# Gates and gated branches of an encoder layer with tokens on partitions, nine of their row pairs as seven products

## The chip, the cores and the metric

The kernel runs on one core of a Trainium2 chip. The core has TensorE (PE in the profile; its weight loads, which overlap its products, are PEld), VectorE (DVE), ScalarE (ACT), GpSimd (POOL) and SyncE (SP), which issues nearly all DMA transfers here. What counts is the device time of one execution in microseconds; a kernel's time is the median of its runs.

## The reference

One layer of an encoder: 256 tokens, 2048 channels, everything in float32.

```python
h = rms_norm(x, norm_mix_pre)
proj = h @ w_in                       # 10240 columns
qa, ka, va, qn, kn, vn, gates = split(proj)     # 6 x 1024 columns, then 2 x 2048 of gates
oa = rms_norm(diff_attention(rope(qa), rope(ka), va)) * (1 - lambda_init)    # [256, 1024]
on = neighbourhood_attention(qn, kn, vn)                                     # [256, 1024]
g_a, g_b = split(sigmoid(gates))                                             # [256, 2048] each
mixed = g_a * (oa @ w_branch_a) + g_b * (on @ w_branch_b)
x = x + rms_norm(mixed @ w_out)
u = square(relu(rms_norm(x) @ w_up))            # 8192 columns
x = x + rms_norm(u @ w_down)
```

The change concerns the lines with gates, g_a, g_b and mixed.

## The kernel before

**Two parts.** Each float32 matrix is two float32r tiles, hi (a cast of it, by ScalarE) and lo (the remainder, by VectorE), and a product is taken as hi·hi + hi·lo + lo·hi. Activations are kept transposed, with channels on the partitions: hT is eight tiles hT0 to hT7 for two 128-row chunks each, every chunk as 256 tokens of hi and then 256 of lo. The attention's results are kept alike, as oaT and onT, eight chunks each. The factor of the row norm, rx, is not in hT; it is multiplied in when a product's result is taken out of PSUM.

**Weights.** load (L94) fetches four 128-row chunks of 512 columns, 1 MB, with one DMA issued by SP, into a raw buffer; split (L101) makes hi (L115, ScalarE) and lo (L116, VectorE) of it in two pieces of 1024 elements a partition. The pool wp has three buffers each for raw, hi and lo. So the next load waits until the remainder of the load three before it has been taken, and a remainder needs its hi first.

**Products.** Two forms are in use. wgroup (L183) holds the weights still and moves the activations: for each 128 of its 512 output columns and each chunk, one product moves hi and lo of the activations past hi of the weights, 512 columns (L191), and one moves hi past lo of the weights, 256 columns (L192). The result is transposed, channels on partitions, in the two halves of a PSUM bank, which halves (L251) adds: ScalarE copies one, VectorE adds the other (L256). agroup (L220) holds the activations still and moves the weights: three products of 512 columns for each chunk and each 128 tokens (L229 to L231). Its result has tokens on the partitions and no halves to add. v of the attention and the output projection use agroup, the down projection the same products (L777 to L779); q, k, gates, branches and the up projection use wgroup. PSUM has eight banks, four under the name mm (large groups) and four under ms (everything else).

**The stage that is changed.** A loop runs over four column groups cg of 512 channels. Each has four wgroup calls: gate a (tiles ga_p, ga_h, ga_l, with the group's number behind ga: 16 chunks, four loads), gate b (gb, the same), branch a (ba: 8 chunks, two loads) and branch b (bb). gate_evac adds the halves, multiplies by rx as a row over all tokens (rxb, L603) and takes the sigmoid (L604); br_evac adds the halves and multiplies with the gate. At the end of a column group the two gated branches are added (L618) and split into mh and ml (L619, L620). They have channels on the partitions, so the output projection's agroup (groups y0 to y3, mstat at L624) uses them as they are.

**Order.** The program is written group by group. advance (L171) puts pieces of the open attention heads between a group's chunks; advance(99) in the loop finishes them. The Tile framework's scheduler then sets each engine's order with a simulated timeline, so that instructions of neighbouring groups mix; each engine, and the queue of SP, takes its own in that order. Tiles come from pools with fixed numbers of buffers: pages (27 of 4 KB a partition) for hT, oaT, onT, gates and the like, wp for weights, tmp for the attention's small tiles (six of 1 KB, seven of 2 KB), tiny, and the two pools of banks.

## Time and profile before

| | |
|---|---|
| median of three runs | 1397.59 us (1396.96 to 1397.92) |
| span of the profiled execution | 1394.5 us |
| stage of gates and branches, first gate product to first product of the output projection | 275.85 us |
| TensorE, VectorE, ScalarE busy | 1374.6 us (99%), 835.8 us (60%), 668.7 us (48%) |
| DMA | 265.16 MB, 190 GB/s on average |
| granted TensorE clock in the stage | 1.00 |

The profiled execution has no time of its own besides its span; the median of the other runs is 3.1 us longer. TensorE's products are pipelined, so a busy TensorE says that products overlapped or followed without a gap, not at what rate; for that, instructions of one kind are counted in a stretch of the span. In a row of the page's groups, "L192 PE MATMUL ga_p<-hT,ga_l" names the line, the engine, the operation, the tile written and the tiles read, then the shape and, behind x, the count, the busy time in us and the mean of one in ns, and last the idle time of the engine before them with what ended it.

### The profile page before, as it was taken

How to read it: one execution, taken by the hardware profiler on the slowest of the kernel's cores; microseconds unless marked ns; L12 is line 12 of the kernel's file. 1: busy time of each engine (PE TensorE's matmuls, PEld its weight loads, DVE VectorE, ACT ScalarE, POOL GpSimd, SP SyncE). 2: the span in 40 equal slices, each digit the busy share in tenths (PEclk: the TensorE clock that was granted, in tenths of full speed). 3: DMA queues.
4: the chain of work that ended last, by engine and by line, in shares of the span. 5: the costliest groups of instructions: out<-in, count | busy, mean ns of one | idle time of the engine just before them, and what ended most of it. 6: DMA issues, size and time to landing. Idle time of an engine off the chain costs nothing.

```text
span 1394.5 us, 17896 instructions
## 1 busy us (share of the span) xinstructions
PE 1374.6 (99%) x7240; PEld 1177.8 (84%) x7240; DVE 835.8 (60%) x1155; ACT 668.7 (48%) x1023; POOL 7.9 (1%) x19
## 2 busy tenths in 40 slices
PE   7999999999999999999899999999999999999997
PEld 6888888888888888888788888888888888888886
DVE  6868866676656565654755555555575554444445
ACT  7554554545444445543744444444464543334332
POOL 0000000000000000000000000000000000000000
PEclk9999999999999999999999999999999999999999
DMA  9674755564555555675455565656555556555551
GB/s 317 202 214 154 202 177 173 171 191 155 165 205 182 203 181 183 203 279 184 149 182 181 182 193 170 211 170 200 189 196 185 203 186 227 195 187 205 181 199 73
DMA packets 117490, 265.16 MB, mean 190 GB/s; under 512 B 15008, under 2 KB 16288, under 8 KB 109216
## 3 DMA queue, kind: packets, MB, share of 16 engines
q1 hardware_dynamic: 117264, 264.03, 57.3%
q8 instruction: 56, 0.92, 0.3%
q14 instruction: 26, 0.21, 0.0%
q10 hardware_dynamic: 144, 0.01, 0.0%
HBM read 261.92 MB, written 3.92 MB: 191 GB/s over the span
## 4 chain that ended last, share of the span: by engine, by line
PE 98%; DVE 1%; DMA 0%; ACT 0%; SPq 0%; issue 0%; DVEq 0%; POOLq 0%; POOL 0%; ACTq 0%
PE u_p L191 17%; PE u_p L192 9%; PE acc L779 8%; PE acc L778 8%; PE acc L777 8%; PE gb_p L191 4%; PE ga_p L191 4%; PE qa_p L191 2%; PE gb_p L192 2%; PE ga_p L192 2%; PE ka_p L191 2%; PE qn_p L191 2%; PE bb_p L191 2%; PE ba_p L191 2%; PE kn_p L191 2%; PE y_p L229 2%
## 5 line engine op out<-in xcount | busy, mean ns | idle before, releaser
L191 PE MATMUL u_p<-h2T,u_h 128*128 128x512 f32 x1024 | 359.9, 398 | 0.5 <-DVE r_m L85 0.5
L192 PE MATMUL u_p<-h2T,u_l 128*128 128x256 f32 x1024 | 284.3, 280 | 0.0
L116 DVE TENSOR_TENSOR d_l<-d_w,d_h 128x1024 fp32r<-128x1024 f32 x128 | 151.1, 1221 | 164.2 <-ACT d_h L115 163.7
L116 DVE TENSOR_TENSOR u_l<-u_w,u_h 128x1024 fp32r<-128x1024 f32 x128 | 151.1, 1222 | 146.0 <-ACT u_h L115 144.7
L191 PEld LDWEIGHTS u_p<-h2T,u_h 128*128 128x128 f32 x1024 | 192.0, 189 | 45.5 <-DVE r_m L85 0.9
L115 ACT CAST d_h<-d_w 128x1024 fp32r<-128x1024 f32 x128 | 128.3, 1052 | 191.1 <-PE acc L779 187.5
L778 PE MATMUL acc<-d_l,uh 128*128 128x512 f32 x512 | 199.0, 389 | 0.0
L779 PE MATMUL acc<-d_h,ul 128*128 128x512 f32 x512 | 198.9, 389 | 0.0
L777 PE MATMUL acc<-d_h,uh 128*128 128x512 f32 x512 | 198.2, 389 | 0.0
L192 PEld LDWEIGHTS u_p<-h2T,u_l 128*128 128x128 f32 x1024 | 193.8, 189 | 1.3
L115 ACT CAST u_h<-u_w 128x1024 fp32r<-128x1024 f32 x128 | 128.0, 1049 | 123.9 <-PE u_p L191 62.5
L778 PEld LDWEIGHTS acc<-d_l,uh 128*128 128x128 f32 x512 | 96.1, 188 | 20.1
L777 PEld LDWEIGHTS acc<-d_h,uh 128*128 128x128 f32 x512 | 96.1, 188 | 20.0
L779 PEld LDWEIGHTS acc<-d_h,ul 128*128 128x128 f32 x512 | 96.1, 188 | 19.8
L191 PE MATMUL gb_p<-hT,gb_h 128*128 128x512 f32 x256 | 90.4, 398 | 0.0
L191 PE MATMUL ga_p<-hT,ga_h 128*128 128x512 f32 x256 | 90.0, 397 | 0.0
L192 PE MATMUL gb_p<-hT,gb_l 128*128 128x256 f32 x256 | 71.4, 281 | 0.0
L192 PE MATMUL ga_p<-hT,ga_l 128*128 128x256 f32 x256 | 70.3, 280 | 0.0
L191 PEld LDWEIGHTS gb_p<-hT,gb_h 128*128 128x128 f32 x256 | 47.9, 188 | 11.5
L116 DVE TENSOR_TENSOR gb_l<-gb_w,gb_h 128x1024 fp32r<-128x1024 f32 x32 | 37.8, 1221 | 31.1 <-ACT gb_h L115 31.1
L191 PEld LDWEIGHTS ga_p<-hT,ga_h 128*128 128x128 f32 x256 | 47.4, 188 | 10.5
L116 DVE TENSOR_TENSOR y_l<-y_w,y_h 128x1024 fp32r<-128x1024 f32 x32 | 37.9, 1222 | 27.8 <-ACT y_h L115 27.8
(213 smaller groups left out, 2348.1 us busy)
## 6 DMA issues: line engine op xcount, KB each, us to landing
u_w<-in_w_up SPq DMA_DIRECT2D x64, 1024.0 KB, 5.4
d_w<-in_w_down SPq DMA_DIRECT2D x64, 1024.0 KB, 4.9
ga_w<-in_w_in SPq DMA_DIRECT2D x16, 1024.0 KB, 5.2
gb_w<-in_w_in SPq DMA_DIRECT2D x16, 1024.0 KB, 5.2
y_w<-in_w_out SPq DMA_DIRECT2D x16, 1024.0 KB, 5.1
ka_w<-in_w_in SPq DMA_DIRECT2D x8, 1024.0 KB, 6.1
va_w<-in_w_in SPq DMA_DIRECT2D x8, 1024.0 KB, 5.2
qn_w<-in_w_in SPq DMA_DIRECT2D x8, 1024.0 KB, 5.1
```

The lines of the kernel that those rows point to most:

```text
L115: nc.scalar.copy(hi[part], raw[part])
L116: nc.vector.tensor_sub(lo[part], raw[part], hi[part].bitcast(F32))
L191: nc.tensor.matmul(ps[b], hi[:, k % 4, cs], mv, start=(k == 0), stop=False)
L192: nc.tensor.matmul(ps[b][:, :T], lo[:, k % 4, cs], mv[:, :T], start=False, stop=(k == nk - 1))
L229: nc.tensor.matmul(ps[t], sh, hi[:, k % 4], start=(k == 0), stop=False)
L777: nc.tensor.matmul(acc[t][c], uh[:, k % 4, ts_], hi[:, 0, cs], start=(k == 0), stop=False)
L778: nc.tensor.matmul(acc[t][c], uh[:, k % 4, ts_], lo[:, 0, cs], start=False, stop=False)
L779: nc.tensor.matmul(acc[t][c], ul[:, k % 4, ts_], hi[:, 0, cs], start=False, stop=(k == NK - 1))
```

## The change

Gates and branches are computed with tokens on the partitions, in two halves h of 1024 columns in place of four groups of 512. A load is now two 128-row chunks of 1024 columns, again 1 MB, a "row pair" i; it is seen as four blocks of 512 columns, [chunk, column half]. pair_weights loads and splits it, in one piece.

- A plain row pair ("eight") takes eight block products, two chunks by two column halves by two token tiles, each with the three products hi·hi, hi·lo, lo·hi of 512 columns: 24. They add up in four banks (1, 2, 3, 7), one for each token tile and column half.
- A "seven" row pair uses the Strassen-Winograd scheme for a 2 by 2 matrix of blocks: seven block products, 21 products on TensorE, of sums of blocks. VectorE adds up the sums of weight blocks (tiles t0 and t1), and they are split as eh0, el0, eh1, el1, in the new pool mid with five buffers. The sums of the blocks of h (tiles hs0, hs3, hs6) are made once by h_sums, in row pairs 4 to 6 of the first group, and used by both gates and both halves. Seven banks take the products; after the last seven row pair of a group combine brings banks 0, 4, 5 and 6 together on ScalarE and VectorE, and piece adds the rest.
- The first group, gate a of half 0, has eight plain row pairs, with the open attention stages between them. The three other gate groups have the order 1, 0 (seven), 2, 3 (seven), 4, 6 (seven), 5, 7: nine seven row pairs in all. Branch groups have four plain row pairs.
- gate_piece and br_piece replace gate_evac and br_evac: no adding of halves, rx as a scale for each partition inside the sigmoid, and passes over a whole bank.
- The mixed rows have tokens on the partitions, so mixed_T turns them, 32 transposes on TensorE through eight banks, and splits them into mh and ml: for half 0 in branch a of half 1, for half 1 after the last branch.
- mid takes the room of tmp, which is closed after the attention and opened anew after the branches.

```diff
-    tmp = ctx.enter_context(tc.tile_pool(name="tmp", bufs=6))
+    temps = ctx.enter_context(ExitStack())
+    tmp = temps.enter_context(tc.tile_pool(name="tmp", bufs=6))
...
+    def pair_weights(view, name, seven):
+        raw = wp.tile([P, 4, 512], F32, tag="raw", name=f"{name}r")
+        last_load[0] = nc.sync.dma_start(raw.rearrange("p (h b) c -> p h (b c)", h=2), view).ins
+        h1, l1 = wtile("hi", f"{name}h"), wtile("lo", f"{name}l")
+        if not seven:
+            nc.scalar.copy(h1, raw)
+            nc.vector.tensor_sub(l1, raw, h1.bitcast(F32))
+            return h1, l1
+        t = [page([P, 2, 512], F32, f"{name}t{i}") for i in range(2)]
+        nc.scalar.copy(h1[:, 1:4], raw[:, 1:4])
+        nc.vector.tensor_add(t[0], raw[:, 1:3], raw[:, 0:1].to_broadcast([P, 2, 512]))
+        nc.vector.tensor_add(t[1][:, 0], t[0][:, 0], raw[:, 2])
+        nc.vector.tensor_add(t[1][:, 1], t[1][:, 0], raw[:, 3])
+        nc.vector.tensor_sub(l1[:, 1:4], raw[:, 1:4], h1[:, 1:4].bitcast(F32))
+        h2, l2 = [], []
+        for i in range(2):
...
+            nc.scalar.copy(h2[i], t[i])
+            nc.vector.tensor_sub(l2[i], t[i], h2[i].bitcast(F32))
+        return h1, l1, h2, l2
+    PLAIN = ((1, 0, 1), (2, 0, 0), (3, 1, 1), (7, 1, 0))
+    class Products:
...
+        def add(self, i, stat, w, blk, last=False):
+            (sh, sl), (wh, wl) = stat, w
+            nc.tensor.matmul(self.ps[i], sh, wh[:, blk], start=i not in self.begun, stop=False)
+            self.begun.add(i)
+            nc.tensor.matmul(self.ps[i], sh, wl[:, blk], start=False, stop=False)
+            nc.tensor.matmul(self.ps[i], sl, wh[:, blk], start=False, stop=last)
+        def seven(self, stat, w, last):
+            r, t = w[:2], list(zip(*w[2:]))
+            self.add(0, stat(0), r, 1, last)
+            self.add(2, stat(6), r, 2)
+            self.add(1, stat(1), r, 3)
+            self.add(4, stat(3), t[0], 0, last)
+            self.add(6, stat(4), t[0], 1, last)
+            self.add(5, stat(5), t[1], 0, last)
+            self.add(3, stat(2), t[1], 1)
+        def eight(self, stat, w, which, last):
+            i, t, half = PLAIN[which]
+            for k in range(2):
+                self.add(i, stat(k, t), w, k * 2 + half, last and k == 1)
+        def combine(self, z):
+            c11, c12, c21, c22 = z[0][:, 1], z[0][:, 0], z[1][:, 1], z[1][:, 0]
+            nc.scalar.copy(c11, self.ps[0])
+            nc.vector.tensor_add(c12, c11, self.ps[5])
+            nc.vector.tensor_add(c21, c12, self.ps[6])
+            nc.vector.tensor_sub(c12, self.ps[4], c12)
+            nc.vector.tensor_sub(c22, self.ps[4], c21)
+    def wide_group(name, kinds, view, stat7, stat8, mm_banks, z, piece, each=None):
...
+        for n, (i, seven) in enumerate(kinds):
+            if each:
+                each(n)
+            w = pair_weights(view(i), f"{name}_{i}", seven)
+            if seven:
+                final = not any(s for _, s in kinds[n + 1 :])
+                pr.seven(partial(stat7, i), w, final)
+                if final:
+                    pr.combine(z)
+                continue
+            end = n == len(kinds) - 1
+            for which in range(4):
+                pr.eight(partial(stat8, i), w, which, end)
+                if end:
+                    b, t, half = PLAIN[which]
+                    piece(t, half, pr.ps[b], any7)
+    def sums_of(p1, p2, name, hi=None, lo=None):
+        a11, a21, a12, a22 = p1[:, :P], p1[:, P:], p2[:, :P], p2[:, P:]
+        s = t2k(f"{name}s").rearrange("p a (b c) -> p (a b) c", b=2)
+        nc.vector.tensor_sub(s[:, 0], a21, a22)
+        nc.vector.tensor_sub(s[:, 1], a11, a21)
+        nc.vector.tensor_sub(s[:, 2], s[:, 0], a11)
+        nc.vector.tensor_add(s[:, 3], a12, s[:, 2])
+        parts_ = page([P, 2, 4, P], F32R, name)
+        nc.scalar.copy(parts_[:, 0], s)
+        nc.vector.tensor_sub(parts_[:, 1], s, parts_[:, 0].bitcast(F32))
+        return parts_
+    def h_sums(i):
+        f = t2k(f"hf{i}")
+        for k in range(2):
+            d = hT[i][:, k].bitcast(F32)
+            nc.vector.tensor_add(f[:, k], d[:, :T], d[:, T:])
+        hsum[i] = sums_of(f[:, 0], f[:, 1], f"hs{i}")
+    def hstat7(i, n):
+        if n < 3:
+            return hstat(i * 2 + (n > 0), n // 2)
+        return hsum[i][:, 0, n - 3], hsum[i][:, 1, n - 3]
...
+    MIXED = [(1, 0), (0, 1), (2, 0), (3, 1), (4, 0), (6, 1), (5, 0), (7, 0)]
+    ALL8 = [(i, 0) for i in range(8)]
...
+    def mixed_T(h, n):
+        mh, ml = page([P, 4, T], F32R, f"mh{h}{n}"), page([P, 4, T], F32R, f"ml{h}{n}")
+        for b in range(2):
+            pt = bank(f"mT{h}{n}{b}")
+            for j in range(2):
+                for t in range(2):
+                    c = (n * 4 + b * 2 + j) * P
+                    nc.tensor.transpose(
+                        pt[:, j * T + t * P : j * T + (t + 1) * P],
+                        mixed[h][t].rearrange("p a b -> p (a b)")[:, c : c + P],
+                        ident,
+                    )
+            at = slice(b * 2, b * 2 + 2)
+            src = pt.rearrange("p (j q) -> p j q", j=2)
+            nc.scalar.copy(mh[:, at], src)
+            nc.vector.tensor_sub(ml[:, at], src, mh[:, at].bitcast(F32))
+        mT.append((mh, ml))
+    for h in range(2):
         gate = []
         for br, gc in (("a", GA), ("b", GB)):
+            z = [page([P, 2, 512], F32, f"g{br}{h}{t}") for t in range(2)]
+            def gate_piece(t, half, ps, summed, z=z):
+                zt = z[t][:, half]
+                if summed:
+                    nc.vector.tensor_add(zt, zt, ps)
+                nc.scalar.activation(
+                    zt, zt if summed else ps, AF.Sigmoid, scale=rx[:, t : t + 1]
+                )
+            first_one = h == 0 and br == "a"
+            def each(n):
+                advance(2)
+                if n >= 4 and n < 7:
+                    h_sums((0, 3, 6)[n - 4])
+            wide_group(
+                f"g{br}{h}",
+                ALL8 if first_one else MIXED,
...
+                each=each if first_one else None,
+            )
+            if first_one:
+                advance(99)
+                temps.close()
+                stage = ctx.enter_context(ExitStack())
+                mid = stage.enter_context(tc.tile_pool(name="mid", bufs=5, reuse_waits="tile"))
+            gate.append(z)
+        for br, src, o, z in (("a", a["w_branch_a"], "a", gate[0]), ("b", a["w_branch_b"], "n", gate[1])):
+            def br_piece(t, half, ps, summed, z=z, br=br, gate=gate):
+                zt = z[t][:, half]
+                nc.vector.tensor_mul(zt, zt, ps)
+                if br == "b":
+                    nc.vector.tensor_add(gate[0][t][:, half], gate[0][t][:, half], zt)
+            wide_group(
+                f"b{br}{h}",
+                ALL8[:4],
...
+                each=(lambda n: mixed_T(0, n // 2) if n in (0, 2) else None) if h and br == "a" else None,
+            )
+        mixed.append(gate[0])
+    for n in range(2):
+        mixed_T(1, n)
+    tmp = temps.enter_context(tc.tile_pool(name="tmp", bufs=6, reuse_waits="tile"))
```

(Comments and docstrings go elsewhere in the file too, so line numbers differ.)

**Where instructions stand now.** Order on TensorE, before, at the start of gate a in column group 1 (ga1_p0 and ga1_p1 are the banks of its first two 128 columns, hT0 and hT1 hold chunks 0 to 3, ga1_0_h and ga1_0_l are the parts of its first load; the last number only counts tiles; rows that read alike are left out):

```order
L191 MATMUL ga1_p0_3667<-hT0_113,ga1_0_h_3673 128x512
L192 MATMUL ga1_p0_3667<-hT0_113,ga1_0_l_3674 128x256
...
L191 MATMUL ga1_p0_3667<-hT1_114,ga1_0_h_3673 128x512
L192 MATMUL ga1_p0_3667<-hT1_114,ga1_0_l_3674 128x256
...
L191 MATMUL ga1_p1_3668<-hT0_113,ga1_0_h_3673 128x512
L192 MATMUL ga1_p1_3668<-hT0_113,ga1_0_l_3674 128x256
```

Order on TensorE, changed kernel, the second half of a seven row pair: row pair 6 of gate b in half 1 (gb14 is bank 4 of group gb1, and so on; gb1_6eh0 and gb1_6el0 are the parts of its first sums of weight blocks; hs6 the sums of h blocks):

```order
L639 MATMUL gb14_4214<-gb1_6eh0_4399,hs6_3291 128x512
L641 MATMUL gb14_4214<-gb1_6el0_4400,hs6_3291 128x512
L642 MATMUL gb14_4214<-gb1_6eh0_4399,hs6_3291 128x512
L639 MATMUL gb16_4216<-gb1_6eh0_4399,hs6_3291 128x512
L641 MATMUL gb16_4216<-gb1_6el0_4400,hs6_3291 128x512
L642 MATMUL gb16_4216<-gb1_6eh0_4399,hs6_3291 128x512
L639 MATMUL gb15_4215<-gb1_6eh1_4403,hs6_3291 128x512
L641 MATMUL gb15_4215<-gb1_6el1_4404,hs6_3291 128x512
L642 MATMUL gb15_4215<-gb1_6eh1_4403,hs6_3291 128x512
```

Where two products of 512 and 256 columns made a pair, three of 512 columns make one block product, and 21 such rows stand for a row pair in place of 24.

Order on VectorE, before, from the end of gate a into gate b of column group 3 (ga3_p0 to ga3_p3 are gate a's banks; gate_s the sum of a bank's halves):

```order
L256 TENSOR_TENSOR gate_s_4991<-ga3_p0_4849,gate_r_4989 128x256
L256 TENSOR_TENSOR gate_s_5005<-ga3_p1_4850,gate_r_5003 128x256
L603 TENSOR_TENSOR gate_s_4991<-gate_s_4991,rxb_122 128x256
L603 TENSOR_TENSOR gate_s_5005<-gate_s_5005,rxb_122 128x256
L256 TENSOR_TENSOR gate_s_5019<-ga3_p2_4851,gate_r_5017 128x256
L603 TENSOR_TENSOR gate_s_5019<-gate_s_5019,rxb_122 128x256
L116 TENSOR_TENSOR gb3_2_l_5125<-gb3_2_w_5122,gb3_2_h_5124 128x1024 x2
L256 TENSOR_TENSOR gate_s_5033<-ga3_p3_4852,gate_r_5031 128x256
L603 TENSOR_TENSOR gate_s_5033<-gate_s_5033,rxb_122 128x256
L116 TENSOR_TENSOR gb3_3_l_5165<-gb3_3_w_5162,gb3_3_h_5164 128x1024 x2
L116 TENSOR_TENSOR ba3_0_l_5233<-ba3_0_w_5230,ba3_0_h_5232 128x1024 x2
L116 TENSOR_TENSOR ba3_1_l_5273<-ba3_1_w_5270,ba3_1_h_5272 128x1024 x2
```

Order on VectorE, changed kernel, in gate b of half 1 (gb1_3, gb1_6 and the like are row pairs; r is the loaded tile, t0 and t1 its sums, l the remainder of its blocks, el0 and el1 those of its sums):

```order
L616 TENSOR_TENSOR gb1_3t1_4323<-gb1_3t1_4323,gb1_3r_4318 128x512
L617 TENSOR_TENSOR gb1_3l_4321<-gb1_3r_4318,gb1_3h_4320 128x1536
L623 TENSOR_TENSOR gb1_3el1_4334<-gb1_3t1_4323,gb1_3eh1_4333 128x1024
L614 TENSOR_TENSOR gb1_6t0_4392<-gb1_6r_4388 128x1024
L610 TENSOR_TENSOR gb1_4l_4361<-gb1_4r_4358,gb1_4h_4360 128x2048
L615 TENSOR_TENSOR gb1_6t1_4393<-gb1_6t0_4392,gb1_6r_4388 128x512
L623 TENSOR_TENSOR gb1_6el0_4400<-gb1_6t0_4392,gb1_6eh0_4399 128x1024
L616 TENSOR_TENSOR gb1_6t1_4393<-gb1_6t1_4393,gb1_6r_4388 128x512
L617 TENSOR_TENSOR gb1_6l_4391<-gb1_6r_4388,gb1_6h_4390 128x1536
L623 TENSOR_TENSOR gb1_6el1_4404<-gb1_6t1_4393,gb1_6eh1_4403 128x1024
L610 TENSOR_TENSOR gb1_5l_4436<-gb1_5r_4433,gb1_5h_4435 128x2048
L610 TENSOR_TENSOR gb1_7l_4466<-gb1_7r_4463,gb1_7h_4465 128x2048
```

Before, remainders alternated with the evacuation of banks. Now a seven row pair puts three adds, a remainder of 1536 elements and two of 1024 into the queue, and the add of row pair 6 (gb1_6t0) stands ahead of the remainder of row pair 4 (gb1_4l), which TensorE uses before it.

Order on TensorE, before, from the last branch group into the output projection (bb3_p3 is the last bank of branch b, y0_p0 the first of the output projection, mh0 and ml0 the mixed parts of column group 0):

```order
L191 MATMUL bb3_p3_5333<-onT6_3297,bb3_1_h_5376 128x512
L192 MATMUL bb3_p3_5333<-onT6_3297,bb3_1_l_5377 128x256
...
L229 MATMUL y0_p0_5470<-y0_0_h_5474,mh0_3661 128x512
L230 MATMUL y0_p0_5470<-y0_0_l_5475,mh0_3661 128x512
L231 MATMUL y0_p0_5470<-y0_0_h_5474,ml0_3662 128x512
```

Order on TensorE, changed kernel, in the first group of the output projection (mT100 to mT111 are the banks of the transposes for half 1, ga10 and ga11 its mixed rows of token tile 0 and 1, mh00 and ml00 the first turned quarter of half 0):

```order
L231 MATMUL y0_p1_4861<-y0_0_l_4865,mh00_4505 128x512
L232 MATMUL y0_p1_4861<-y0_0_h_4864,ml00_4506 128x512
L741 MATMUL mT100_4795<-ident_80,ga10_3915 128x128
L741 MATMUL mT101_4802<-ident_80,ga10_3915 128x128
L741 MATMUL mT110_4811<-ident_80,ga10_3915 128x128
L741 MATMUL mT111_4818<-ident_80,ga10_3915 128x128
L230 MATMUL y0_p1_4861<-y0_0_h_4864,mh00_4505 128x512
L741 MATMUL mT110_4811<-ident_80,ga11_3916 128x128
...
L741 MATMUL mT111_4818<-ident_80,ga11_3916 128x128
```

The output projection starts on the turned rows of half 0, and the transposes of half 1 stand between its products.

More of the change, by code (lines that the diff above doesn't have):

```diff
@@ new lines, in encoder_layer, with __init__ @@
+    PLAIN = ((1, 0, 1), (2, 0, 0), (3, 1, 1), (7, 1, 0))
+    class Products:
+        def __init__(self, name, mm_banks, used=range(8)):
+            self.ps = {i: bank(f"{name}{i}", i in mm_banks) for i in used}
+            self.begun = set()
+        def add(self, i, stat, w, blk, last=False):
[24 more added lines that the diff above has]
+            nc.vector.tensor_sub(c22, self.ps[4], c21)
```

51 lines of the change are left out of this document (31 added, 20 removed).

## The prediction

> **What bounds the kernel now.** I read the page first, then who made TensorE wait, then the stretch that the change touches.
>
> ```profile
> span 1394.5 us, 17896 instructions
> ...
> PE 1374.6 (99%) x7240; PEld 1177.8 (84%) x7240; DVE 835.8 (60%) x1155; ACT 668.7 (48%) x1023; POOL 7.9 (1%) x19
> ...
> PE 98%; DVE 1%; DMA 0%; ACT 0%; SPq 0%; issue 0%; DVEq 0%; POOLq 0%; POOL 0%; ACTq 0%
> ```
>
> TensorE is busy for 99% of the span and is 98% of the chain of work that ended last. The view of waits lists everything that TensorE waited for:
>
> ```profile
> PE hT_t L268 <- DMA x<-in_x: 6.0, 2, 3.9
> PE h2T_t L664 <- DVE x L657: 3.2, 1, 3.2
> PE qa_p L191 <- DVE hT L274: 1.2, 1, 1.2
> PE u_p L191 <- DVE r_m L85: 0.5, 1, 0.5
> ```
>
> The tiles hT_t and qa_p belong to the start and h2T_t and u_p to the step into the MLP; none belongs to gates or branches. So the time of that stage is its number of products times the spacing at which they follow each other. Busy times are no guide to that, since products overlap; the view by stretches is (columns: length, then busy time and instructions of PE, PEld, DVE, ACT, POOL, clock, DMA share, GB/s).
>
> ```profile
> 305.10:580.95 275.85, 275.85 (x1591) 240.85 (x1589) 176.92 (x257) 136.90 (x218) 0.00 (x0) 1.00 0.53 180
> 449.00:516.40 67.40, 67.40 (x385) 58.63 (x384) 42.53 (x59) 32.68 (x49) 0.00 (x0) 1.00 0.55 187
> 1047.00:1380.00 333.00, 333.00 (x1471) 275.74 (x1470) 158.45 (x137) 134.80 (x142) 0.00 (x0) 1.00 0.54 186
> ```
>
> The first row is the whole stage, from the first gate product to the first product of the output projection: 275.85 us. The second is one of its four column groups, without attention in it: 192 pairs (one product of 512 columns, one of 256) in 67.4 us, 0.3510 us a pair. The third is the down projection, which has the form that the changed stage gets, three products of 512 columns: 333.0 / 1471 = 0.2264 us each. All 768 pairs of the stage are 269.6 us; the remaining 6.2 are the attention heads still running there.
>
> **The change part by part.** *Products.* The 768 pairs go (-269.6 us). Without the sums there would be 48 row pairs of 24 products, 1152; nine of them need 21, so 1125 products of 512 columns come: 1125 x 0.2264 = 254.7. The form alone gives 269.6 - 1152 x 0.2264 = 8.8 us, the sums 27 x 0.2264 = 6.1.
>
> *Transposes.* With tokens on partitions the mixed rows must be turned for the output projection: 32 new transposes, in eight banks of four. The trace has such a bank between products:
>
> ```profile
> 317.67 0.28 PE L192 MATMUL ga_p<-hT,ga_l 128*128 128x256 f32 x1
> 317.79 0.60 PE L424 MATMUL n_pt<-ident,np 128*128 128x128 f32 x4
> 318.15 0.48 PE L191 MATMUL ga_p<-hT,ga_h 128*128 128x512 f32 x1
> 318.47 0.28 PE L192 MATMUL ga_p<-hT,ga_l 128*128 128x256 f32 x1
> ```
>
> Four take 0.36 us, and the product behind them 0.32 instead of 0.23: 0.45 a bank, 3.6 in all. All of it is on the path.
>
> *Work of VectorE and ScalarE.* It costs nothing as long as TensorE's products cover it; here is how far they do.
>
> ```profile
> L116 DVE TENSOR_TENSOR gb_l<-gb_w,gb_h 128x1024 fp32r<-128x1024 f32 x32 | 37.8, 1221 | 31.1 <-ACT gb_h L115 31.1
> ...
> L115 ACT CAST gb_h<-gb_w 128x1024 fp32r<-128x1024 f32 x32 | 32.0, 1047 | 25.4 <-PE gb_p L191 13.7 <-issue 10.3 <-ACT ga L604 0.8
> ...
> L256 DVE TENSOR_TENSOR gate_s<-gb_p,gate_r 128x256 f32<-128x256 f32 x16 | 6.4, 419 | 0.0
> ...
> L809 DVE TENSOR_TENSOR zw<-acc,gp 128x512 f32<-128x512 f32 x8 | 5.3, 688 | 6.2 <-ACT jd L807 5.9
> ...
> L371 ACT CAST n_pT<-n_pt 128x512 fp32r<-128x512 f32 x8 | 4.4, 584 | 0.0
> ```
>
> VectorE takes 0.42, 0.69 and 1.22 us for 256, 512 and 1024 elements, a line of 1.04 ns an element; carried on, 1536 are 1.75 and 2048 are 2.29 (estimates). ScalarE: 0.58 and 1.05, so 1.48 and 1.90. A plain row pair is one remainder of 2048: VectorE 2.29 against 24 x 0.2264 = 5.43 on TensorE. A seven-product row pair has adds of 1024, 512 and 512, a remainder of 1536 and two of 1024: 1.22 + 2 x 0.69 + 1.75 + 2 x 1.22 = 6.79, against 21 products, 4.75. So VectorE alone is the slower one there, by 2.04. A mixed group (five plain, three seven) with its combination and evacuation, eight passes of 0.69 over a bank, is 11.5 + 20.4 + 5.5 = 37.4 against 183 x 0.2264 = 41.4: VectorE is at 90%, and keeps up on average only. ScalarE has 5 x 1.90 + 3 x 3.58 + 0.58 + 4 x 0.6, about 23. Branch groups lighten both: the two-halves evacuation (a copy, an add, a multiplication of 256 each) becomes one pass of 512 over each bank.
>
> *Queues.* What counts is order, since VectorE takes its instructions in turn. I followed its queue through the three mixed groups by hand. The tightest place is gb1, which follows another mixed group at once. Its row pair 6 starts its adds ahead of the remainder of row pair 4, and these adds wait for a load. That load is issued when the remainder of row pair 2 has freed its buffer; this takes:
>
> ```profile
> first_w<-in_w_in SPq DMA_DIRECT2D x2, 1024.0 KB, 10.1
> ...
> gb_w<-in_w_in SPq DMA_DIRECT2D x16, 1024.0 KB, 5.2
> ```
>
> Counted from the first product of gb1: the evacuation of ga1 still occupies VectorE to 5.3, a sum's remainder to 6.5, the remainder of row pair 2 to 8.8; the load of 6 lands at 14.0; its add of 1024 ends at 15.2, the remainder of 4 at 17.5. TensorE has row pairs 1, 0, 2 and 3 before it, 90 products, 20.4 us. It arrives 2.9 us after the data. By the same count the slack is about 4 us in ga1 and 5 in gb0 (whose VectorE has the row sums of h behind it, 3 x 2.7 us, done under ga0's 43 us of products). So no wait, and I cost this at nothing; what would take the cover away is a load of more than 5.2 + 2.9 = 8.1 us. The DMA queue issues as many loads of 1 MB as before: one per 5.43 us in plain row pairs and 4.75 in seven-product ones, against 5.6 before (67.4 us for the 12 loads of a column group); at most 18% faster, so 0.65 of the DMA engines' time where the second row above shows 0.55.
>
> *Banks.* Combination reads four banks under the two plain row pairs that end a group (10.9 us for 4 x 0.69); each of the other four is evacuated 1.4 us after the one before, in 0.69, and the next group comes to the first of them 4.1 us later. Nothing. *Into the output projection.* The last mixed quarter is ready 3.4 us after the last branch product (0.69 for each multiplication and add left, and one remainder of 1024); TensorE has 26 products of y0 on the first two quarters before the first transpose, 5.9 us. The turned tiles are needed 2.2 us and more after the transposes end and take 0.58 + 0.68. Nothing; if that cover is gone the price is once 1 to 3 us.
>
> *Other parts.* The sums' parts in the attention's room (pools tmp and mid): first used by gb0 some 10 us after the last head stage; nothing. Everything ahead of the first gate product keeps its order, and behind y0 only neighbours change places: nothing.
>
> *Sum*: 254.7 + 3.6 + 6.2 = 264.5 against 275.85: -11.3. On this execution's span 1394.5 gives 1383.2; the median of the runs, 1397.59, lies 3.1 above the span, and with the same 3.1 the time is 1386.3.
>
> Bounds of the unknown terms. Spacing: 0.2264 is a mean over 1471 products in a stage with the same kind of loads and of VectorE work; the slowest stretch of that form is the first of the output projection:
>
> ```profile
> 580.95 0.40 PE L229 MATMUL y_p<-y_h,mh 128*128 128x512 f32 x1
> ...
> 581.19 0.40 PE L230 MATMUL y_p<-y_l,mh 128*128 128x512 f32 x1
> ...
> 582.82 0.40 PE L231 MATMUL y_p<-y_h,ml 128*128 128x512 f32 x1
> ```
>
> Eight products in 1.87, 0.234 each, or +8.6 us over 1125: an end of the range, not the value. Transposes: 2.9 (0.36 a bank) to 4.5. Waits: 0 to 2 us a mixed group if loads take first_w's 10.1 (10.1 - 8.1), so 0 to 6.
>
> **The rivals.** *The form is worth nothing*: what a product costs goes by its columns alone. A pair is 768 columns in 0.3510, so 512 would be 0.2340, and the stage 263.3 + 3.6 + 6.2 = 273.1: -2.8, 1394.8. The bound above speaks for it, for 2 us; all 1471 products of the down projection speak against. The Trainium skill says nearly this in "TensorE: Matmul & The Clock Gate", section "Back-to-back issue gap": in isolation a warm product follows the last after N / 2.4 GHz + 2.5 ns. By its figures a pair is 0.325 and a 512 is 0.2158, so 768 pairs are 249.6 and 1125 products 242.8; with 32 transposes at 0.056 (1.8) its estimate is -5.0 us, 1392.6. The trace disagrees: the pair loses 26 ns on that figure where the 512 loses 11.
>
> *VectorE's queue costs part of it*: TensorE waits at a remainder or a sum in each mixed group, 1 to 3 us each. For it: 90% load, adds placed ahead of remainders. Against: 2.9 us and more of slack. Price 3 to 8: 1389 to 1394.
>
> *Slower, by VectorE setting the pace of the sums*: if the lead of about two row pairs that three buffers give is used up from the start, a seven-product row pair takes VectorE's 6.79 instead of 4.75: 9 x 2.04 = 18.4, 1404.7. It decides once TensorE waits more than 11.3 + 2.8 = 14.1 us in the three mixed groups, 4.7 in each. Against it: before every mixed group but gb1 there is a group in which VectorE needs under 15 us of TensorE's 21.7 or about 41 of 51.
>
> **How the numbers follow.** From no change this kernel's measurement tells about 0.2%, 2.8 us. Forecast 0.70 (1384.5 to 1389); queue costs part of it 0.17; form worth nothing 0.07; VectorE sets the pace 0.06. Faster: 0.70, nearly all of 0.17 and a fifth of the 0.07: 0.88. Same: 0.06; slower 0.06. The range takes in the low transposes and a spacing of 0.2250 (-2.3) below, and the second case nearly whole above: 1383.5 to 1393.
>
> **What would show it.** The stretch from the first gate product to the first of y0 is 264.5 us and holds 1125 products of 512; three in a row span 0.68; TensorE's waits name no tile of gates or branches; ga1 and gb1 are 41.4 us each with VectorE near 37 busy. Wrong if the waits name remainders or sums (h, l, eh, el), or if the products stand 0.23 and more apart.

## The result, and the profile after

The changed kernel takes 1385.61 us (median of four runs, 1385.37 to 1386.53) against 1397.53 us before (four runs, 1396.96 to 1397.92): a ratio of 0.9917, 95% interval 0.9905 to 0.9929. That is 11.9 us less; 11.3 were forecast. The profiled execution of the changed kernel took 1386.53 us, 1.8 more than its span. The two profiled spans, 1394.5 and 1384.7, are only 9.8 apart: the changed stretches below are 11.1 us shorter, the opening of this execution was 2.1 longer, and the rest 0.8 shorter.

The page of the changed kernel, its parts that answer to those of before:

```profile
span 1384.7 us, 16956 instructions
...
PE 1363.7 (98%) x6861; PEld 1157.6 (84%) x6861; DVE 851.7 (62%) x1093; ACT 659.6 (48%) x923; POOL 7.9 (1%) x19
...
PE 98%; DVE 1%; DMA 0%; ACT 0%; SPq 0%; issue 0%; DVEq 0%; POOLq 0%; POOL 0%; ACTq 0%
```

The view of waits, all that TensorE waited for (us in total, times, longest):

```profile
PE hT_t L269 <- DMA x<-in_x: 6.9, 2, 3.8
PE h2T_t L860 <- DVE x L853: 3.2, 1, 3.2
PE qa_p L192 <- DVE hT L275: 1.2, 1, 1.2
PE u_p L192 <- DVE h2T L870: 1.0, 1, 1.0
```

TensorE is still the bound, and no tile of gates or branches is among its waits. So the stage's time is again products times spacing. The view by stretches (columns as in the prediction), first from the first gate product to the first product of the output projection, then from there to the first of the up projection, then both together; then the groups gb of half 0, ga and gb of half 1:

```profile
307.17:570.17 263.00, 263.00 (x1195) 218.85 (x1194) 192.86 (x196) 128.41 (x119) 0.00 (x0) 1.00 0.57 190
570.17:664.99 94.82, 90.65 (x414) 74.65 (x412) 53.01 (x68) 42.65 (x69) 1.10 (x2) 1.00 0.63 210
307.17:664.99 357.82, 353.65 (x1608) 293.49 (x1606) 245.87 (x262) 171.06 (x188) 1.10 (x2) 1.00 0.59 196
...
357.13:398.39 41.26, 41.26 (x184) 34.17 (x182) 33.05 (x28) 22.16 (x18) 0.00 (x0) 1.00 0.61 204
441.91:483.39 41.48, 41.48 (x185) 34.36 (x183) 36.05 (x34) 21.98 (x17) 0.00 (x0) 1.00 0.59 203
483.39:524.87 41.48, 41.48 (x184) 34.31 (x183) 32.41 (x29) 20.73 (x17) 0.00 (x0) 1.00 0.62 203
```

The same stretches of the kernel before:

```profile
305.10:580.95 275.85, 275.85 (x1591) 240.85 (x1589) 176.92 (x257) 136.90 (x218) 0.00 (x0) 1.00 0.53 180
580.95:674.00 93.05, 89.34 (x399) 73.38 (x397) 53.14 (x67) 42.61 (x69) 1.10 (x2) 0.99 0.63 215
305.10:674.00 368.90, 365.19 (x1987) 314.23 (x1985) 230.06 (x323) 179.51 (x286) 1.10 (x2) 1.00 0.56 189
```

Half of the transposes stand behind the first product of the output projection, so the stage is 1.5 us shorter than the 264.5 forecast, and the second stretch is 1.8 longer than before. Together they went from 368.90 to 357.82, 11.08 less. The groups of 183 products take 41.3 to 41.5 us where 41.4 were forecast (41.48 / 183 = 0.2267 a product), with VectorE busy for 32 to 36: it does 7 to 9 us of a mixed group's work on weights before the group's first product. A bank's worth of transposes in the timeline, between gate b of half 1 and branch a (columns: start, length, engine, line, operation):

```profile
524.64 0.39 PE L642 MATMUL gb<-gb_7h,hT 128*128 128x512 f32 x1
524.87 1.03 PE L741 MATMUL mT<-ident,ga 128*128 128x128 f32 x8
525.66 0.48 PE L639 MATMUL ba<-ba_0h,oaT 128*128 128x512 f32 x1
525.98 0.40 PE L641 MATMUL ba<-ba_0l,oaT 128*128 128x512 f32 x1
```

Two banks take 0.79 us, and the product behind them 0.32 instead of 0.23: 0.44 a bank; 0.45 was taken.

VectorE's queue in gate b of half 1, the place called the tightest, with SP's issue of the load of row pair 6, and TensorE's first use of row pairs 0 and 4 where it needs a remainder (rows of VectorE, of SP's queue and of TensorE):

```profile
481.94 1.76 DVE L617 TENSOR_TENSOR gb_0l<-gb_0r,gb_0h 128x1536 fp32r<-128x1536 f32 x1
...
487.24 0.39 PE L641 MATMUL gb<-gb_0l,hT 128*128 128x512 f32 x1
...
488.28 2.29 DVE L610 TENSOR_TENSOR gb_2l<-gb_2r,gb_2h 128x2048 fp32r<-128x2048 f32 x1
...
490.60 0.37 SPq L606 DMA_DIRECT2D gb_6r<-in_w_in  x1
...
495.68 1.22 DVE L614 TENSOR_TENSOR gb_6t<-gb_6r 128x1024 f32<-128x1024 f32 x1
496.81 2.29 DVE L610 TENSOR_TENSOR gb_4l<-gb_4r,gb_4h 128x2048 fp32r<-128x2048 f32 x1
...
503.79 0.39 PE L639 MATMUL gb<-gb_4h,hT 128*128 128x512 f32 x1
504.01 0.39 PE L641 MATMUL gb<-gb_4l,hT 128*128 128x512 f32 x1
```

The remainder of row pair 2 ends at 490.57, and the load of row pair 6 is issued then. It lands 5.0 us later, just before VectorE has finished its work on row pair 3 and comes to the add at 495.68, so the load holds nothing up. The remainder of row pair 4 ends at 499.10. Counted from the group's first product at 483.39 that is 15.7 us; 17.5 were forecast. TensorE comes at 20.4, as forecast. The slack is 4.7 us instead of 2.9.

It is not the smallest of the group. The scheduler mixed the products of neighbouring row pairs, and the remainder of row pair 0, ready at 483.70, is used at 487.24: 3.5 us. In the branch groups, which the prediction did not follow, the remainder of the second row pair is ready 2.6 to 3.5 us before its use (397.40 and 399.97 in branch a of half 0).

**The opening.** The first gate product came 2.1 us later than in the profile of before, though the order ahead of it is the same. The second block of transposes of x waited 0.97 us longer for its transfer, and TensorE ran slowly for longer. Rows of the timeline, before:

```profile
7.10 1.11 PE L268 MATMUL hT_t<-ident,x 128*128 128x128 f32 x4 [2.06 <-DMA x<-in_x]
...
11.49 0.63 PE L191 MATMUL qa_p<-hT,qa_h 128*128 128x512 f32 x1
...
14.77 0.40 PE L191 MATMUL qa_p<-hT,qa_h 128*128 128x512 f32 x1
```

and after:

```profile
7.94 1.12 PE L269 MATMUL hT_t<-ident,x 128*128 128x128 f32 x4 [3.03 <-DMA x<-in_x]
...
12.34 0.63 PE L192 MATMUL qa_p<-hT,qa_h 128*128 128x512 f32 x1
...
16.88 0.40 PE L192 MATMUL qa_p<-hT,qa_h 128*128 128x512 f32 x1
```

Between 10 and 20 us TensorE gets through 43 instructions where it did 55 before; a pair of products takes 0.64 us early in that stretch and 0.35 later. The Trainium skill says in "TensorE: Matmul & The Clock Gate", section "Part 1: The HAM clock gate", that the first stretch of work runs at half rate and that its length varies between runs of the same kernel. That would fit; the profile's clock column shows 1.00 there and cannot settle it. The thirteen profiles here, all of kernels with the same opening, have their first gate product between 304.7 and 307.2 us, the changed kernel's two at 307.2 and 306.1. So the 2.1 us lie within what executions of one opening differ by.

### The profile page after: what moved, and what is told of

Same layout as the page of the kernel before. It is cut to its first block, busy times and chain, and to the rows that moved or that the text cites. A ratio compares the mean times of both kernels' runs of the same rounds, so it can differ in the third digit from the quotient of the medians.

```text
span 1384.7 us, 16956 instructions
## 1 busy us (share of the span) xinstructions
PE 1363.7 (98%) x6861; PEld 1157.6 (84%) x6861; DVE 851.7 (62%) x1093; ACT 659.6 (48%) x923; POOL 7.9 (1%) x19
## 4 chain that ended last, share of the span: by engine, by line
PE 98%; DVE 1%; DMA 0%; ACT 0%; SPq 0%; issue 0%; DVEq 0%; POOLq 0%; POOL 0%; ACTq 0%
PE u_p L192 17%; PE u_p L193 9%; PE acc L975 8%; PE acc L974 8%; PE acc L973 8%; PE qa_p L192 2%; PE ka_p L192 2%; PE qn_p L192 2%; PE kn_p L192 2%; PE ga L639 2%; PE y_p L232 2%; PE y_p L231 2%; PE ga L642 2%; PE ga L641 2%; PE y_p L230 2%; PE gb L642 2%
## 5 line engine op out<-in xcount | busy, mean ns | idle before, releaser
L116 ACT CAST y_h<-y_w 128x1024 fp32r<-128x1024 f32 x32 | 32.0, 1047 | 40.9 <-PE y_p L232 32.6
L230 PE MATMUL y_p<-y_h,mh 128*128 128x512 f32 x128 | 50.1, 391 | 0.0
L231 PE MATMUL y_p<-y_l,mh 128*128 128x512 f32 x128 | 49.9, 390 | 0.0
L232 PE MATMUL y_p<-y_h,ml 128*128 128x512 f32 x128 | 49.8, 390 | 0.0
L192 PE MATMUL qa_p<-hT,qa_h 128*128 128x512 f32 x128 | 47.7, 419 | 1.2 <-DVE hT L275 1.2
L192 PE MATMUL qn_p<-hT,qn_h 128*128 128x512 f32 x128 | 45.9, 400 | 0.0
L192 PE MATMUL kn_p<-hT,kn_h 128*128 128x512 f32 x128 | 45.4, 398 | 0.0
```

The lines of the kernel that those rows point to most:

```text
L116: nc.scalar.copy(hi[part], raw[part])
L192: nc.tensor.matmul(ps[b], hi[:, k % 4, cs], mv, start=(k == 0), stop=False)
L230: nc.tensor.matmul(ps[t], sh, hi[:, k % 4], start=(k == 0), stop=False)
L231: nc.tensor.matmul(ps[t], sh, lo[:, k % 4], start=False, stop=False)
L232: nc.tensor.matmul(ps[t], sl, hi[:, k % 4], start=False, stop=(k == nk - 1))
```

## The experiments

The length of a stretch tells more than the time of a run: the two profiles of the changed kernel give 357.82 and 357.79 us for both stretches together, while the runs of one kernel differ by 1 to 3 us, and the experiments ran on three chips. Theory: only TensorE's products count, and VectorE's work for the sums is covered. Rivals: VectorE's queue takes part of the gain; a product costs by its columns alone. The first two runs take away one term of the sum each.

**All row pairs plain.** The sums of weights and of h, and the combination, are left out with them:

```diff
-    MIXED = [(1, 0), (0, 1), (2, 0), (3, 1), (4, 0), (6, 1), (5, 0), (7, 0)]
+    MIXED = [(1, 0), (0, 0), (2, 0), (3, 0), (4, 0), (6, 0), (5, 0), (7, 0)]
...
-                if n >= 4 and n < 7:
-                    h_sums((0, 3, 6)[n - 4])
```

> The changed kernel with 24 products in every row pair: no sums of weight blocks, no sums of h, no combination. It has 1152 products of 512 columns in the stage. My theory (TensorE's products at 0.2264 us each are all that counts, and VectorE's work for the sums is wholly covered): 27 products more than the changed kernel, +6.1 us, about 1391.7, and still 5.2 to 6 us faster than before (the form 8.8 less 3.6 for the transposes). Rival, VectorE's queue costs part of the sums' gain: less than +6.1, say +3 to +4, and less waiting or a closer spacing in the trace. Rival, a product costs by its columns alone: about 1397, no faster than before.

Measured: 1392.17 us, ratio to before 0.9966 (0.9952 to 0.9979). Its stretches, the stage and then both:

```profile
305.26:574.49 269.23, 269.23 (x1222) 223.82 (x1221) 136.05 (x106) 111.86 (x95) 0.00 (x0) 1.00 0.56 186
...
305.26:669.30 364.04, 359.88 (x1634) 298.45 (x1632) 189.05 (x173) 154.59 (x164) 1.10 (x2) 1.00 0.58 192
```

364.04 against 357.82: the 27 products are worth 6.2 us, the whole of what they cost, so the sums take nothing back. The last rival (no faster than before) is refuted: the plain form alone makes the two stretches 4.9 us shorter.

**Mixed rows not turned.**

```diff
-            pt = bank(f"mT{h}{n}{b}")
...
-                    nc.tensor.transpose(
...
-            src = pt.rearrange("p (j q) -> p j q", j=2)
+            src = mixed[h][b][:, n].rearrange("p (j q) -> p j q", j=2)
```

> The changed kernel without the 32 transposes: mh and ml are taken straight from the mixed rows, so the output projection gets them unturned and its result is not the layer's; all other work stays. My theory: eight banks at 0.45 us lie on TensorE's path, so 3.6 us less than the changed kernel, about 1382.0, half of it before the first product of the output projection and half behind it. Rival, the last quarter's turn also costs a wait in the output projection: 5 to 7 us less. Rival, the transposes hide in the gaps between products: no difference.

Measured: 1382.5 us, ratio 0.9896 (0.9882 to 0.9909). Both stretches together:

```profile
305.16:659.32 354.16, 350.31 (x1575) 290.38 (x1574) 245.77 (x262) 171.73 (x188) 1.10 (x2) 1.00 0.59 198
```

357.82 - 354.16 = 3.7 us for the 32 transposes; 3.6 were forecast, all of it on the path, and no wait goes with them. With this the form follows: 364.04 - 3.7 is 8.5 us less than 368.90.

**A seven row pair first in each mixed group.**

```diff
-    MIXED = [(1, 0), (0, 1), (2, 0), (3, 1), (4, 0), (6, 1), (5, 0), (7, 0)]
+    MIXED = [(0, 1), (1, 0), (3, 1), (2, 0), (6, 1), (4, 0), (5, 0), (7, 0)]
```

> The three mixed groups in the order 0 (seven), 1, 3 (seven), 2, 6 (seven), 4, 5, 7: a seven row pair stands first, right behind the evacuation of the group before. Number of products and all work unchanged. My theory: the sums of row pair 0 (6.8 us on VectorE) must be done beside the last plain row pairs of the group before, its combination and its evacuation; in 10.9 us of TensorE's products VectorE then has 2.3 + 2.8 + 6.8 and part of the 2.8 of evacuation, 12 to 14 us, so TensorE waits 0 to 3 us at the start of each mixed group, 0 to 6 in all (1385.5 to 1391.5), and the waits name the parts of row pair 0. Rival, the covers are larger than I counted: no difference, under 0.5 us. Rival, order decides: more than 8 us slower.

Measured: 1386.36 us, ratio 0.9922 (0.9910 to 0.9934). The stage:

```profile
305.95:568.95 263.00, 263.00 (x1196) 218.77 (x1194) 193.47 (x196) 128.98 (x119) 0.00 (x0) 1.00 0.56 190
```

263.00 as in the changed kernel: the rival with larger covers is right, and this other place in the group does not matter with three of eight. The waits of TensorE again name no tile of the stage.

**Five seven row pairs in each mixed group.**

```diff
-    MIXED = [(1, 0), (0, 1), (2, 0), (3, 1), (4, 0), (6, 1), (5, 0), (7, 0)]
+    MIXED = [(1, 0), (0, 1), (2, 1), (3, 1), (4, 1), (6, 1), (5, 0), (7, 0)]
...
-        return hsum[i][:, 0, n - 3], hsum[i][:, 1, n - 3]
+        u = hsum[i if i in hsum else 6]
+        return u[:, 0, n - 3], u[:, 1, n - 3]
```

> Five instead of three seven row pairs in each mixed group, in the order 1, 0, 2, 3, 4, 6 (the five behind 1 are seven), 5, 7; for row pairs 2 and 4 the sums of h of row pair 6 stand in, so the output is not the layer's. Per group TensorE has 177 products, 40.1 us (41.4 with three); VectorE has 3 x 2.29 + 5 x 6.79 + 5.5 = 46.3 us (37.4 with three). My theory (VectorE is hidden up to its rate and sets the pace beyond it): 18 products less, -4.1 us, but waits of up to 6.2 us in a mixed group, less what VectorE is ahead at its start; in sum 2 to 14 us slower than the changed kernel, 1387.5 to 1399.5, and TensorE's waits name parts of weights. Rival, VectorE's load does not matter even here: 4.1 faster, 1381.5, and no such waits.

Measured: 1387.65 us, ratio 0.9934 (0.9921 to 0.9946), 2.0 above the changed kernel's median, though the kernel before was 0.9 faster beside this run. Both stretches together are 358.99 us, 1.2 above, which is the surer number. So 5.3 us were lost against 4.1 saved: VectorE does set the pace, and by this number the result is a little under the 2 to 14 us that I expected. The waits and the groups ga and gb of half 1:

```profile
PE gb L641 <- DVE gb_0l L617: 1.1, 1, 1.1
PE gb L641 <- DVE gb_6l L617: 1.0, 1, 1.0
...
PE gb L641 <- DVE gb_4l L617: 0.5, 1, 0.5
PE gb L639 <- DVE ga L761: 0.2, 1, 0.2
```

```profile
439.34:479.73 40.39, 40.39 (x178) 33.07 (x177) 38.10 (x38) 20.34 (x16) 0.00 (x0) 1.00 0.62 209
479.73:524.88 45.15, 42.34 (x183) 33.02 (x182) 43.14 (x43) 26.40 (x25) 0.00 (x0) 1.00 0.53 178
```

With 46 us of work against 40 of products, gate a of half 1 has no wait: VectorE had done 10.3 us of its work on weights beside the branch group ahead. Gate b, which follows it at once, began with 3.5 us of its own done, and holds nearly the whole loss: 45.15 less 40.1 for 177 products and 0.4 for a bank of transposes, 4.6 us. The view of waits lists 2.8; it counts only time with no product open, and each is open 0.16 us beyond the spacing, so short waits do not show.

**Four seven row pairs**, with the sums of row pair 6 standing in for those of 4 as above:

```diff
-    MIXED = [(1, 0), (0, 1), (2, 0), (3, 1), (4, 0), (6, 1), (5, 0), (7, 0)]
+    MIXED = [(1, 0), (0, 1), (3, 1), (2, 0), (4, 1), (6, 1), (5, 0), (7, 0)]
```

> Four seven row pairs in each mixed group, in the order 1, 0 (seven), 3 (seven), 2, 4 (seven), 6 (seven), 5, 7; for row pair 4 the sums of h of row pair 6 stand in, so the output is not the layer's. Nine products less, -2.0 us; VectorE has 41.9 us a group against 40.8 of TensorE's products, an excess of 1.1 us a group. Theory (VectorE is hidden as long as it is ahead, and only gb1, behind another mixed group, uses its lead up): stage 2.0 us less than in the changed kernel, no wait in gb0 and ga1 and at most 1 us in gb1, about 1384. Rival, VectorE sets the pace at its rate in every group: 3.4 us of waits, 1.4 slower than the changed kernel.

Measured: 1383.82 us, ratio 0.9904 (0.9889 to 0.9919). The stage:

```profile
305.67:566.72 261.05, 261.05 (x1186) 217.04 (x1185) 204.42 (x211) 132.66 (x125) 0.00 (x0) 1.00 0.56 191
```

1.95 less, and no wait: a total above 100% for VectorE in three groups is covered while it is ahead.

**Four with the right sums of h, second sums inside the loaded tile.**

```diff
-        t = [page([P, 2, 512], F32, f"{name}t{i}") for i in range(2)]
+        t = [page([P, 2, 512], F32, f"{name}t0"), raw[:, 0:2]]
...
-        nc.vector.tensor_add(t[1][:, 0], t[0][:, 0], raw[:, 2])
-        nc.vector.tensor_add(t[1][:, 1], t[1][:, 0], raw[:, 3])
+        nc.vector.tensor_add(raw[:, 0], t[0][:, 0], raw[:, 2])
         nc.vector.tensor_sub(l1[:, 1:4], raw[:, 1:4], h1[:, 1:4].bitcast(F32))
+        nc.vector.tensor_add(raw[:, 1], raw[:, 0], raw[:, 3])
...
```

> As the run with four seven row pairs, but with the right sums of h for row pair 4. There is no page left for them, so the second sums of weight blocks go into the blocks of the loaded tile that are no longer used (block 0 after the first add, block 1 after the remainder), which frees a page. It computes the layer. Theory: the loaded tile is held longer, by the last add and the remainder of the second sums, some 2 us a seven row pair; the load takes 5 us and three buffers cover it, so the time is that of the run before, about 1384, 2.0 us less than the changed kernel. Rival, the later load is missed in gb1: 1 to 3 us of waits there, nothing gained.

Measured: 1388.01 us, ratio 0.9929 (0.9917 to 0.9942); both stretches 360.17 us, 4.3 above the run before and 2.4 above the changed kernel. The rival is right, and the loss is more than it said. Waits of TensorE, and in VectorE's timeline its wait for the load of row pair 4 in gate b of half 1:

```profile
PE ba L641 <- DVE ba_2l L610: 1.6, 1, 1.6
...
PE gb L639 <- DVE ga L760: 0.8, 1, 0.8
PE gb L639 <- ACT gb_5h L609: 0.6, 1, 0.6
```

```profile
497.19 1.23 DVE L614 TENSOR_TENSOR gb_4t<-gb_4r 128x1024 f32<-128x1024 f32 x1 [2.58 <-DMA gb_4r<-in_w_in]
```

The tile held longer makes the loads late in gate b of half 1. That of row pair 4 is issued 12.6 us after the group's first product (at 492.36), where it was 5.9 in the run before; VectorE stands idle for 2.6 us, and what TensorE needs comes late in this group and in the branch group behind it.

**Four, four and three.** The second sums go into the loaded tile only in gate b of half 0 and gate a of half 1; gate b of half 1 keeps the changed kernel's order and pages.

```diff
...
-                ALL8 if first_one else MIXED,
+                ALL8 if first_one else FOUR if (h, br) in ((0, "b"), (1, "a")) else MIXED,
```

> Four seven row pairs in gate b of half 0 and gate a of half 1, with the second sums inside the loaded tile as in the run before; gate b of half 1 keeps three, in the order and with the pages of the changed kernel. It computes the layer. Theory (a wait arises only in the mixed group that directly follows another, and behind it): six products less than the changed kernel, stage 1.4 us less and no waits on parts of weights, about 1384.3. Rival, holding the loaded tile longer costs wherever it is done: waits of 1 us and more remain, 1385.5 or above.

Measured: 1384.81 us, ratio 0.9912 (0.9897 to 0.9927). The stage is 262.26 us, 0.7 less than in the changed kernel where 1.4 were expected; one wait of 0.3 us is left (gate b of half 1 on a bank's evacuation, L766). Gate b of half 0 and gate a of half 1 take 40.80 us each, what 180 products take, so the tile held longer costs nothing there; gate b of half 1 is 0.6 us longer than in the changed kernel. The theory has the place right, and missed that even three seven row pairs there lose something.

**Four in all three groups with 27 pages and nothing else changed:**

```diff
-    MIXED = [(1, 0), (0, 1), (2, 0), (3, 1), (4, 0), (6, 1), (5, 0), (7, 0)]
+    MIXED = [(1, 0), (0, 1), (3, 1), (2, 0), (4, 1), (6, 1), (5, 0), (7, 0)]
...
-                if n >= 4 and n < 7:
-                    h_sums((0, 3, 6)[n - 4])
+                if n >= 4:
+                    h_sums((0, 3, 6, 4)[n - 4])
```

> Four seven row pairs in all three mixed groups with the right sums of h for row pair 4 and no other change: all tiles as in the changed kernel, so the sums of weight blocks have one page less and wait for one where 27 are not enough. It computes the layer. Theory: the stage needs at most one page more than there are, and the sums of one row pair start a little later; 2.0 us less than the changed kernel if VectorE's lead covers that, about 1383.8. Rival, the missing page holds VectorE's queue up in gb1 as the longer held tile did: 2 to 4 us of waits, 1386 to 1388.

Measured: 1384.74 us, ratio 0.9909 (0.9892 to 0.9925), beside 1386.08 us for the changed kernel on the same chip. The stage:

```profile
306.92:567.97 261.05, 261.05 (x1186) 217.10 (x1185) 206.56 (x218) 133.15 (x126) 0.00 (x0) 1.00 0.57 191
```

The theory holds: the missing page costs nothing in the stage, which is as long as with the wrong sums of h. So the 4.3 us lost two runs ago belong to the second sums in the loaded tile. This version has the shortest stage of those that compute the layer. Its median and the changed kernel's differ by 1.3 us and their intervals overlap; the 1.95 us in the stage are the surer number.

**The changed kernel again.**

> The changed kernel itself, beside the two others on the same chip, and a second profile of its opening. If the 2.1 us by which its first gate product came later than before (307.2 against 305.1) belong to the execution and not to the kernel, the first gate product is at 305 to 306 here, while the stage to the first product of the up projection is again 357.8 us.

Measured: 1386.08 us, ratio 0.9919 (0.9904 to 0.9933). The first gate product is at 306.07, at the edge of what I expected and 1.1 us earlier than in the first profile of the same kernel; both stretches are 357.79 us, as expected:

```profile
306.07:663.86 357.79, 353.78 (x1607) 293.44 (x1605) 245.85 (x262) 171.32 (x188) 1.10 (x2) 1.00 0.59 195
```

**Where the gain of the form lies.** Two runs for the disputed price of a product. First, the kernel before with the 256-column product of gates and branches widened:

```diff
+            w = 2 * T if name[0] in "gb" else T
             nc.tensor.matmul(
-                ps[b][:, :T], lo[:, k % 4, cs], mv[:, :T], start=False, stop=(k == nk - 1)
+                ps[b][:, :w], lo[:, k % 4, cs], mv[:, :w], start=False, stop=(k == nk - 1)
```

> The kernel before, with the 256-column product of each pair in gates and branches widened to 512 columns (low part of the weights by both parts of the activations): 768 pairs of two products of 512 columns with the weights still. It tells where the 8.8 us of the form come from. Theory, the loss belongs to the products of 256 columns (a pair takes 0.3510, a 512 product 0.2264, so the 256 one 0.1246): now 0.2264 each, 0.453 a pair, stage 78.2 us longer, 354. Rival, the loss belongs to holding the weights still (the 512 product itself follows at 0.235 there): 0.470 a pair, stage 91 us longer, 367.

Measured: one run of 1474.17 us; stage 354.37 us.

```profile
304.70:659.07 354.37, 354.37 (x1590) 294.25 (x1589) 181.76 (x260) 140.69 (x220) 0.00 (x0) 1.00 0.42 140
```

Less 6.2 for attention, 348.2 / 1536 = 0.2267 us a product with the weights still: as much as with the activations still (261.15 / 1152 = 0.2267 in the plain form, less 6.2 for attention and 1.8 for half of the transposes). So it is not holding the weights still that costs, but the products of 256 columns. Second, the changed kernel with one product in three split:

```diff
-            nc.tensor.matmul(self.ps[i], sh, wl[:, blk], start=False, stop=False)
+            for c in (slice(0, 256), slice(256, 512)):
+                nc.tensor.matmul(self.ps[i][:, c], sh, wl[:, blk, c], start=False, stop=False)
```

> The changed kernel with the second of the three products of each block product (high part of the activations by low part of the weights) split into two of 256 columns: 1125 products of 512 become 2250 of 256, the other 2250 thirds stay. Theory, the loss belongs to products of 256 columns: each costs 0.1246 in place of half of 0.2264, 22.8 ns more for each split product; 1125 / 3 = 375 of them are split, so the stage is 8.6 us longer. Rival, the loss belongs to the other form: 256 columns cost half of 512, no difference.

(375 products become 750; the middle of that text counts wrongly, its last sentence rightly.) Measured: one run of 1392.08 us; stage 269.31 us.

```profile
306.31:575.62 269.31, 269.31 (x1570) 235.94 (x1569) 193.11 (x196) 128.49 (x119) 0.00 (x0) 1.00 0.55 186
```

6.3 us more, 16.8 ns for each split product, 8.4 for each product of 256; the pair of before loses 0.3510 - 1.5 x 0.2267 = 11 ns for its one. The rival of no difference is refuted; the price is three quarters of the expected. Why the short product is dear stays open. Each product has a load of its own for the operand held still (PEld), 0.19 us long in the profile's records whatever the columns, and a product follows one of 256 columns by about 0.12 us. No run here separates a load that the short product does not cover from a cost of the short product itself.

## Why the prediction was right, and where it was not

- *What bounds the kernel*: right. TensorE has no wait in the stage, before or after.
- *Products and form*: forecast -8.8, shown -8.5 (plain form, less the transposes). The spacing came out at 0.2267 in place of 0.2264. What the form saves, which the prediction read from the spacings alone, is the short product: 768 x 11 ns = 8.4 us.
- *Sums*: forecast -6.1, shown -6.2. *Transposes*: forecast +3.6, shown +3.7. *Both stretches*: forecast -11.3, shown -11.1.
- *Queues*: right that nothing waits, and right about the group (gate b of half 1), not about the row pair. The slack of row pair 4 was counted at 2.9 us and is 4.7: VectorE had finished the evacuation of gate a by 3.8 us after the group's start, not 5.3, and all that follows moves with it. The smallest in the group is 3.5 us, at row pair 0, since TensorE does not take whole row pairs in turn; the prediction's own count left only 1.4 at row pair 2 (ready at 8.8, used after 45 products at 10.2). With five seven row pairs the loss falls on that group, and the longest wait is for the remainder of row pair 0.
- *ScalarE's times*: the estimates 1.48 and 1.90 us do not follow from 0.58 and 1.05, which give 1.51 and 1.97. Measured are 1.48 and 1.91, so nothing hangs on it.
- *The rival that VectorE sets the pace*: its rate is right, its condition was not. It was priced at 9 x 2.04 for three seven row pairs a group, as if VectorE could not run ahead; even with five of them only 5.3 us were lost in place of up to 18.6 (three groups at 6.2), since it works ahead beside the branch groups.
- *The rival by columns alone*: refuted by the widened product. The Trainium skill's isolated figure ("TensorE: Matmul & The Clock Gate", section "Back-to-back issue gap") gives an estimate of 0.2158 for 512 columns; in three forms of the stage 0.2267 was measured, 11 ns more. For 256 columns the same formula gives an estimate of 0.1092, and a pair leaves 0.3510 - 0.2267 = 0.1243, 15 ns more.
- *Span and median*: the number was right, its reading was not. The 3.1 us by which the median of before lay above the profiled span are not one constant: each execution here takes 1.7 to 1.9 us more than its own span, and the other 1.3 come from the profiled execution of before, which was a fast one (spans of that kernel run from 1394.2 to 1397.6). The forecast is unharmed, since adding 3.1 to the span less 11.3 is the same as taking 11.3 from the median. The median of before less the measured 11.1 would be 1386.4, and 1385.6 and 1386.1 were measured, within what executions differ by. So the 11.9 us between the medians hold about 11.1 that are shown in the stretches; the rest is not shown to belong to the change.
- *Everything else at nothing*: right within 1 us, apart from the opening. With the same code, the opening ends anywhere within 2.5 us and the up projection takes 362.5 to 364.1 us in these profiles, so smaller effects there could not be seen.

## What to carry to other kernels

Where one engine has no wait, count its instructions by form and spacing in a stretch of its own, and a change of form can be priced to a few tenths of a microsecond. In these runs, work that a second engine took over was free as long as that engine could run ahead, even where a group of it needed more than the group's time; the loss came in the group that follows another such group, since there the lead is used up. Compare spans with spans and times with times.

## What was not expected of the hardware

In these runs a product of 256 columns among products of 512 cost 8 to 11 ns more than half a product of 512, whichever operand was held still (0.3510 us a pair against 0.3401 by columns; 0.2267 for 512). And the same opening varied by 2.5 us over thirteen executions of programs that share it, more than the last step to four seven row pairs (1.95 us) was worth.
